# A bidirectional encoder layer: VectorE in place of GpSimd, four more products early, another order of products, and v loaded earlier

## The chip, the cores and the metric

The kernel runs on one core of a Trainium2 chip. The time is device microseconds of one execution; lower is better. The core's engines work at the same time, each through a queue of its own: TensorE (PE) multiplies matrices, VectorE (DVE), ScalarE (ACT) and GpSimd (POOL) do elementwise work, and SyncE (SP) issues most DMAs; POOL issues others. PE writes to PSUM, which has eight banks here: four under the name "g", four under "d".

## The reference

One layer on 1024 tokens of width 1024, all in float32:

```
h = x + 1/2 * SwiGLU_1(RMSNorm(x))                # d_ff 2816
u = RMSNorm(h)
[qA|kA|vA|qB|kB|vB|gA|gB] = u @ W_in
yA = NeighbourhoodAttention2D(qA, kA, vA)         # 8 heads, learned bias
yB = WindowedGQA(rope(qB), rope(kB), vB)          # 8 heads, 2 of k and v, sink logit
h = h + (sigmoid(gA)*(yA @ W_A) + sigmoid(gB)*(yB @ W_B)) @ W_out
h = h + 1/2 * SwiGLU_2(RMSNorm(h))
y = RMSNorm_final(h)
```

Scores of qA, kA and qB, kB are scaled by 0.125.

## The kernel before

**Arithmetic.** Each float32 operand is split into a high part (a ScalarE cast to fp32r, line 88) and a low part (a subtraction, line 89, by VectorE unless another engine is named). One product of such operands is three matmuls: high by high, high by low, low by high (`mm3`, lines 137 to 144).

**Products in Strassen form.** The gate and up projections of both FFNs and most of W_in are computed with seven products P1 to P7 in place of eight. The right-hand sides B11, B21, T2, T1, B22, T3 and T4 come from the normalized, transposed activations: T1 = B12 - B11, T2 = B22 - T1, T3 = T2 - B11, T4 = B21 - T2. In `to_strassen` (lines 188 to 218) token tiles 0 to 3 give B11 and B21, tiles 4 to 7 give B22, T1 and T2, and the corners that become T3 and T4, which `strassen_rest` (220 to 225) splits at the end. Of T1 the low part, and the two corner subtractions (lines 210, 211), are on GpSimd.

**`products`** (232 to 330) runs over groups i of output columns (11 for an FFN, 5 for W_in); in a group each product is done for m = 0 and 1 (gate and up, or two chunk pairs of W_in). A step (i, p, m) is four yields of three matmuls. W, X and Y are the PSUM banks of a group: P1, P6, P7, P4 add up in W, P2 in X, P5 and P3 in Y. Between them `after` copies or adds the banks out. `prep` loads and splits the left-hand side; `prep_until` sets how far ahead. P1 and P2 of group 1 are taken early, behind those of group 0, since they need only B11 and B21; `load_ahead` loads their weights. `hidden` (344 to 388) is the FFN's `after`, with SwiGLU and the left-hand sums of the down projection, written to DRAM by POOL DMAs; `store_z` (598 to 632) is that of W_in, which writes z to DRAM.

**Transitions.** `transition` (159 to 178) norms and transposes tile by tile; after tile t its `post(t - 1)` runs some yields of the early products (`behind`, 332 to 342: seven each from t = 3 on). There are three: before FFN1, before W_in (the mix stage), before FFN2. `fetch` (264 to 267) multiplies the weights of qA and qB (column chunks 0 to 3 and 12 to 15 of W_in) by 0.125 on GpSimd.

**Hooks.** In the W_in stage `at_end(n)` calls what is hooked to n products before the end: five `rope` steps (640 to 655: two `xs` buffers, loads from z, three VectorE operations, a POOL DMA) and `v_b` (657 to 668: loads v of B from z into an `xs` buffer and transposes it on PE). There are two `xs` buffers.

The order in each engine's queue is made at build time: instructions are taken as the builder thinks their inputs ready, earlier lines first.

Of the kernel before, what the change touches and what calls it, by code (L numbers as in the profile page):

```python
# [15 lines left out]
P = 128  # L16
# [20 lines left out]
def trunk_kernel(ctx, tc, x, n1, wg1, wu1, wd1, nm, win, rpb, sink, wa, wb, wo,  # L37
# [150 lines left out]
    def to_strassen(t, xs):  # L188

        pa, pb = turned(xs)  # L190
        tt = t % 4
        cols = slice(tt * P, (tt + 1) * P)

        def put(o, src, eng=None):
            h, l = rhs(o)
            split(h[:, :, cols], l[:, :, cols], src, eng)

        x11 = res(tt)[:, :512].rearrange("p (c t) -> p c t", c=4)
        x21 = res(tt)[:, 512:].rearrange("p (c t) -> p c t", c=4)
# [9 lines left out]
        nc.vector.tensor_tensor(t2, pb, t1, op=ALU.subtract)  # L209
        nc.gpsimd.tensor_tensor(x11, t2, x11, op=ALU.subtract)  # L210
        nc.gpsimd.tensor_tensor(x21, x21, t2, op=ALU.subtract)
        put(T2, t2)
        put(B22, pb)
        put(T1, t1, nc.gpsimd)
        if kept:
            x12 = main.tile([P, 512], F32, tag="s1", bufs=1, name=nm_("s1"))
            nc.scalar.copy(x12.rearrange("p (c t) -> p c t", c=4), pa)
            nc.sync.dma_start(kept[0][t - 4], x12)

    def strassen_rest():  # L220
        for o, k in ((T3, 0), (T4, 512)):
            h, l = rhs(o)
            for tt in range(4):
                cols = slice(tt * P, (tt + 1) * P)
                split(h[:, :, cols], l[:, :, cols], res(tt)[:, k:k + 512].rearrange("p (c t) -> p c t", c=4))
# [6 lines left out]
    def products(src, n, after, at_end, extra, ring, scaled=lambda i, m, half: False):  # L232

        seq = [(i, p, m) for i in range(n) for p in PRODUCTS for m in range(2)]
        early = [(1, p, m) for p in ("P1", "P2") for m in range(2)]
# [19 lines left out]
        def load_ahead():  # L258

            for m in range(2):  # L260
                ahead[m] = main.tile([P, 1024], F32, tag="ws", bufs=8, name=nm_("ahead"))
                fetch(ahead[m], 1, m, 0)

        def fetch(r, i, m, half):
            nc.sync.dma_start(r.rearrange("p (c f) -> p c f", f=P), src(i, m, half))
            if scaled(i, m, half):
                nc.gpsimd.tensor_scalar_mul(r, r, 0.125)

        def prep(q):
            if q >= len(seq):  # L270
                return
            i, p, m = seq[q]
            if (i, p, m) in early:
                w = lhs[q] = ws4()
                c0 = 512 if p == "P2" else 0
                split(w[:, :512], w[:, 512:], ahead[m][:, c0:c0 + 512])
                return
            for half in range(2):
                if (i, m, half) not in raws:
                    load(i, m, half)  # L280
            r1, r2 = raws[i, m, 0], raws[i, m, 1]
            a11, a12, a21, a22 = r1[:, :512], r1[:, 512:], r2[:, :512], r2[:, 512:]
            s1 = None
            if p == "P5":
                s1 = main.tile([P, 512], F32, tag="s1", bufs=1, name=nm_("s1"))
                nc.vector.tensor_tensor(s1, a21, a22, op=ALU.add)
            elif p == "P3":
                nc.vector.tensor_tensor(a12, a12, a11, op=ALU.subtract)
            w = ws4()
            split(w[:, :512], w[:, 512:], dict(P1=a11, P2=a12, P5=s1, P6=a11, P7=a21, P3=a12, P4=a22)[p])  # L290
            if p == "P5":
                nc.vector.tensor_tensor(a21, a11, a21, op=ALU.subtract)
                nc.vector.tensor_tensor(a11, s1, a11, op=ALU.subtract)
            lhs[q] = w

        def multiply(q):
# [13 lines left out]
            for c in range(4):  # L310
                cs = slice(c * P, (c + 1) * P)
                mm3([b], c == 0 and p in ("P1", "P2", "P5"), c == 3, (w[:, cs], w[:, 512:][:, cs]),
# [10 lines left out]
        def run():  # L323
            for q in range(len(seq)):
                prep_until(q + 1 if q < 4 else q + 8)
                yield from multiply(q)
                after(*seq[q], bks[seq[q][0]], snap[seq[q][0]], sn)
# [4 lines left out]
    def behind(prods):  # L332
# [3 lines left out]
        def post(t):  # L336
            if t >= 3:
                drain(run, 7)
# [5 lines left out]
    def hidden(wg, wu, at_end):  # L344
# [4 lines left out]
        def after(i, p, m, bks, snap, sn):  # L349
            if p in ("P1", "P6"):  # L350
                c = snap["11" if p == "P1" else "21", m] = sn()
                nc.scalar.copy(c, bks["W", m])
            elif p == "P5":
                c = snap["22", m] = sn()
                nc.scalar.copy(c, bks["Y", m])
            elif p == "P4":
                if m == 0:
                    snap["12"] = sn()
                    nc.scalar.activation(snap["12"], bks["W", 0], AF.Silu)
                    return  # L360
                a12, s4 = snap["12"], snap["21", 0]
                nc.vector.tensor_tensor(a12, bks["W", 1], a12, op=ALU.mult)
                put(i, "P2", a12)
                nc.vector.tensor_tensor(s4, a12, snap["21", 1], op=ALU.subtract)
                put(i, "P3", s4)
            else:
# [6 lines left out]
                g = snap[key, 0]  # L373
                nc.vector.tensor_tensor(g, c, g, op=ALU.mult)  # L374
                if p != "P3":
                    put(i, "P1" if p == "P2" else "P4", g)
                    return
                a11, a22 = snap["11", 0], snap["22", 0]
                s1, s2, s3 = snap["22", 1], c, snap["11", 1]
                nc.vector.tensor_tensor(s1, g, a22, op=ALU.add)  # L380
                put(i, "P5", s1)
                nc.vector.tensor_tensor(s2, s1, a11, op=ALU.subtract)
                put(i, "P6", s2)
                nc.vector.tensor_tensor(s3, a11, g, op=ALU.subtract)
                put(i, "P7", s3)
# [190 lines left out]
    drain(transition(res, gain, to_strassen, behind(hg), spare=(2, 3)))  # L576
# [21 lines left out]
    def store_z(i, p, m, bks, snap, sn):  # L598
# [9 lines left out]
        def put(ch, n, c):  # L608
            if ch < 12:
                parts = [(z_d, c)]  # L610
                if ch < 8:
                    hl = [main.tile([P, 512], F32R, tag="hs", bufs=4, name=nm_("hs")) for _ in range(2)]
                    split(hl[0], hl[1], c)
# [11 lines left out]
        if p in ("P1", "P5", "P6", "P4"):  # L625
            c = snap[key, m] = sn()
            nc.scalar.copy(shaped(c, ch), view(bks[src, m], ch))
        else:
            c = snap[key, m]
            nc.vector.tensor_tensor(shaped(c, ch), view(bks[src, m], ch), shaped(c, ch), op=ALU.add)  # L630
# [25 lines left out]

    def v_b():
        mix["vb"] = [new_fx(k, F32R).rearrange("p (t d) -> p t d", t=NTT) for k in (0, 1)]
        r = xs4()
        nc.sync.dma_start(r, z_d[17 * P:18 * P, :])  # L660
# [75 lines left out]
    for c in range(4):  # L736
        hook(14 * (NG - 1) - 2 - 3 * c, rope, c)
    hook(14 * (NG - 2) - 2, rope, 4)
    hook(14 * (NG - 2) - 12, v_b)
# [6 lines left out]
                  lambda i, m, half: groups[i][m][half] in (0, 1, 2, 3, 12, 13, 14, 15))  # L746
# [454 lines left out]
```

## Time and profile before

| | |
|---|---|
| median of 3 runs | 1987.9 us (1984.55 to 1991.54) |
| profiled execution, span | 1987.6 us |
| mean granted TensorE clock | 0.993 |
| DMA | 290.31 MB, 146 GB/s |
| PE, DVE, ACT, POOL busy | 98%, 72%, 48%, 21% of the span |

An engine's busy time counts the time in which at least one instruction of it was in work; matmuls overlap. A row of the windows view gives length, busy time and instruction count of PE, PE's weight loads, DVE, ACT and POOL, the granted clock as a share of the full one, and the DMA engines' share and rate. A row of waits names who waited for whom: total us, times, longest. A row of groups names line, engine, operation, what is written from what, count, busy us and mean ns, then idle time before it and who ended that. FFN1's transition and products fill about 0 to 440 us, the W_in stage about 640 to 870, FFN2's transition and products about 1320 to 1740; down projections and attention lie between.

### The profile page before, as it was taken

To read this page: it belongs to the slowest core of one execution; us is meant where nothing else is said; L and a number is where in the kernel's file an instruction comes from. 1 tells how busy PE (TensorE), PEld (TensorE's weight loads), DVE (VectorE), ACT (ScalarE), POOL (GpSimd) and SP (SyncE) were. 2 spreads that over 40 slices of the span, in tenths; PEclk is the share of its full clock that TensorE was granted. 3 is DMA by queue.
4 is the path that set the end of the run, shared out by engine and by line. 5 is a ranking of instruction groups with operands and counts; after the bars stand their busy time and mean duration, and the time that the engine had idled before them with its cause. 6 is when DMAs were issued, how large, how long until landed. Compare 5 with 4: busy or idle time off the path is not lost.

```text
span 1987.6 us, 25701 instructions
## 1 busy us (share of the span) xinstructions
PE 1938.4 (98%) x8968; PEld 1612.7 (81%) x8968; DVE 1439.8 (72%) x2495; ACT 957.4 (48%) x1857; POOL 422.0 (21%) x474
## 2 busy tenths in 40 slices
PE   6999999999999999999999999998999999999998
PEld 5788888888888778788888888887888888888886
DVE  7866566558967677768889866999656656659864
ACT  7433333334446443468777873365333333344453
POOL 4101001002500533311112134513101100105100
PEclk9999999999999999999999999999999999999999
DMA  6423323367233469973357675544332342393341
GB/s 194 147 85 106 121 92 106 108 220 277 84 121 125 145 160 243 201 174 107 87 143 173 172 253 195 179 147 127 120 114 88 105 126 85 125 349 129 108 140 62
DMA packets 257217, 290.31 MB, mean 146 GB/s; under 512 B 46880, under 2 KB 187552, under 8 KB 257088
## 3 DMA queue, kind: packets, MB, share of 16 engines
q1 hardware_dynamic: 200576, 203.09, 32.8%
q0 software_dynamic: 56512, 85.58, 15.2%
q8 instruction: 71, 1.16, 0.2%
q14 instruction: 58, 0.48, 0.1%
HBM read 202.01 MB, written 86.70 MB: 145 GB/s over the span
## 4 chain that ended last, share of the span: by engine, by line
PE 82%; DVE 8%; issue 4%; DMA 3%; POOL 2%; ACT 2%; SPq 0%; POOLq 0%; DVEq 0%; ACTq 0%
PE g L140 16%; PE g L142 16%; PE g L144 16%; PE d L140 10%; PE d L142 10%; PE d L144 10%; PE d L991 2%; DVE ws L89 2%; DVE ar L89 1%; DMA xs<-z_d 1%; PE d L970 1%; PE d L971 1%; PE g L1010 1%; PE g L1005 1%; DVE ar L1116 1%
## 5 line engine op out<-in xcount | busy, mean ns | idle before, releaser
L140 PE MATMUL g<-ar,ws 128*128 128x512 f32 x1208 | 455.7, 398 | 9.2 <-ACT ar L88 3.5
L142 PE MATMUL g<-ar,ws 128*128 128x512 f32 x1208 | 448.6, 392 | 3.7 <-DVE ar L89 3.7
L144 PE MATMUL g<-ar,ws 128*128 128x512 f32 x1208 | 447.3, 392 | 2.1 <-DVE ws L89 2.0
L89 DVE TENSOR_TENSOR ws<-raw,ws 128x512 fp32r<-128x512 f32 (+1 forms) x335 | 249.5, 748 | 189.6 <-ACT ws L88 188.4
L88 ACT CAST ws<-raw 128x512 fp32r<-128x512 f32 (+1 forms) x337 | 213.3, 638 | 272.6 <-PE d L144 108.5
L142 PEld LDWEIGHTS g<-ar,ws 128*128 128x128 f32 x1208 | 228.4, 189 | 52.0 <-DVE ar L89 4.4
L144 PEld LDWEIGHTS g<-ar,ws 128*128 128x128 f32 x1208 | 228.3, 189 | 51.7 <-DVE ws L89 3.2
L140 PEld LDWEIGHTS g<-ar,ws 128*128 128x128 f32 x1208 | 223.0, 189 | 51.9 <-ACT ar L88 4.7
L140 PE MATMUL d<-ar,ws 128*128 128x512 f32 x656 | 254.3, 392 | 4.7 <-DVE ar L89 4.7
L142 PE MATMUL d<-ar,ws 128*128 128x512 f32 x656 | 254.2, 391 | 0.0
L144 PE MATMUL d<-ar,ws 128*128 128x512 f32 x656 | 254.0, 391 | 0.0
L347 POOL DMA_DIRECT2D hid<-fx x98 | 53.1, 542 | 501.1 <-DVE fx L374 364.6
L140 PEld LDWEIGHTS d<-ar,ws 128*128 128x128 f32 x656 | 124.1, 189 | 31.4 <-issue 5.5
L144 PEld LDWEIGHTS d<-ar,ws 128*128 128x128 f32 x656 | 124.1, 189 | 25.9
L142 PEld LDWEIGHTS d<-ar,ws 128*128 128x128 f32 x656 | 124.0, 189 | 25.9
L89 DVE TENSOR_TENSOR ws<-ar,ws 128x512 fp32r<-128x512 f32 x114 | 109.1, 964 | 6.7 <-ACT ws L88 6.7
L89 DVE TENSOR_TENSOR ws<-fa,ws 128x512 fp32r<-128x512 f32 x80 | 55.3, 691 | 63.5 <-ACT ws L88 63.1
L88 ACT CAST ar<-raw 128x512 fp32r<-128x512 f32 (+1 forms) x83 | 56.0, 679 | 93.1 <-PE g L142 51.1
L140 PE MATMUL g<-ws,ws 128*128 128x512 f32 x232 | 90.9, 392 | 0.0
L142 PE MATMUL g<-ws,ws 128*128 128x512 f32 x232 | 90.4, 390 | 0.0
L144 PE MATMUL g<-ws,ws 128*128 128x512 f32 x232 | 90.3, 389 | 0.0
L978 ACT ACTIVATE fa<-fa,nmx 128x385 f32<-128x385 f32 (+3 forms) x128 | 75.5, 591 | 26.9 <-DVE nmx L975 26.2
(222 smaller groups left out, 3588.3 us busy)
## 6 DMA issues: line engine op xcount, KB each, us to landing
raw<-hid SPq DMA_DIRECT2D x70, 512.0 KB
hid<-fx POOLq DMA_DIRECT2D x98, 256.0 KB, 2.4
raw<-in_ffn_w_up_dram SPq DMA_DIRECT2D x32, 512.0 KB
ar<-in_ffn_w_down_dram SPq DMA_DIRECT2D x32, 512.0 KB
raw<-in_ffn_w_gate_dram SPq DMA_DIRECT2D x28, 512.0 KB
hid<-fa POOLq DMA_DIRECT2D x56, 256.0 KB, 2.7
raw<-in_w_in_dram SPq DMA_DIRECT2D x27, 512.0 KB
ar<-zs_d POOLq DMA_DIRECT2D x48, 256.0 KB, 5.0
```

The lines of the kernel that those rows point to most:

```text
L88: nc.scalar.copy(dst_hi, src)
L89: (eng or nc.vector).tensor_tensor(dst_lo, src, f32v(dst_hi), op=ALU.subtract)
L140: nc.tensor.matmul(b, lhs[0], r[0], start=first, stop=False, **kw)
L142: nc.tensor.matmul(b, lhs[0], r[1], start=False, stop=False, **kw)
L144: nc.tensor.matmul(b, lhs[1], r[0], start=False, stop=last, **kw)
L347: nc.gpsimd.dma_start(hid[PRODUCTS.index(p), i], src)
L970: nc.tensor.matmul(b[:, :nw], un["q"][s], un["kd"][s][:, k0 * P:k1 * P], start=True, stop=False)
L971: nc.tensor.matmul(b[:, :nw], un["q"][s], un["kl"][s][:, k0 * P:k1 * P], start=False, stop=True)
L978: nc.scalar.activation(pr, pr, AF.Exp, scale=-1.0, bias=nmx[:, s:s + 1], accum_out=ssum[:, s:s + 1])
L991: nc.tensor.transpose(pt[:, i * P:(i + 1) * P], un["pr"][s][:, i * P:(i + 1) * P], ident)
L1005: nc.tensor.matmul(o[:, s], un["v"][s][:, un["k0"] + i, :], un["p"][s][:, i], start=i == 0, stop=i == last)
L1010: nc.tensor.matmul(o, un["v"][0][:, un["k0"] + i, :], un["p"][k][:, i], start=i + k == 0, stop=i + k == last + 1)
```

## The change

- `to_strassen`: T1's low part and the corners go to VectorE; T1 is split first; corners of tiles 6 and 7 wait for `strassen_rest`.
- P3 comes before P7 (in the last group of W_in the old order stays); `hidden` builds its sums in the matching order.
- P1 and P2 of group 2 ("merged") are early too. They add up in one X bank; P1 alone is copied to a buffer `u`, and W then starts at P6, so that `u` is added where P6, P5 and P4 are read.
- `behind` runs 6, 9, 9, 8, 16 yields (FFN1: 7, 7, 7, 7, 20), 48 for the twelve early products; before it was 7 each, with 32 for eight.
- Splits run three products ahead at first and up to eight later; before, one ahead for four products, then eight at once.
- The factor 0.125 is taken at eviction, by ScalarE's scale or a VectorE operation with a scalar.
- v of B is loaded by a hook of its own, 14 products before its transposes; hooks move.

```
-        nc.gpsimd.tensor_tensor(x11, t2, x11, op=ALU.subtract)
-        nc.gpsimd.tensor_tensor(x21, x21, t2, op=ALU.subtract)
+        put(T1, t1)
         put(T2, t2)
         put(B22, pb)
-        put(T1, t1, nc.gpsimd)
+        if t < 6:
+            corners(tt)
...
+    def corners(tt):
+        x11, x21, t2 = res(tt)[:, :512], res(tt)[:, 512:], res(tt + 4)[:, 512:]
+        nc.vector.tensor_tensor(x11, t2, x11, op=ALU.subtract)
+        nc.vector.tensor_tensor(x21, x21, t2, op=ALU.subtract)
+
     def strassen_rest():
+        for tt in (2, 3):
+            corners(tt)
...
-    PRODUCTS = ("P1", "P2", "P5", "P6", "P7", "P3", "P4")
+    PRODUCTS = ("P1", "P2", "P5", "P6", "P3", "P7", "P4")
...
-        early = [(1, p, m) for p in ("P1", "P2") for m in range(2)]
+        early = [(i, p, m) for i in (1, MERGED) for p in ("P1", "P2") for m in range(2)]
...
+            for m in range(2):
+                for k, p in enumerate(("P1", "P2")):
+                    r = ahead[MERGED, p, m] = main.tile([P, 512], F32, tag="hs", bufs=4, name=nm_("ahead"))
+                    nc.sync.dma_start(r.rearrange("p (c f) -> p c f", f=P), src(MERGED, m, 0)[:, 4 * k:4 * k + 4, :])
...
-            if scaled(i, m, half):
-                nc.gpsimd.tensor_scalar_mul(r, r, 0.125)
...
-            if p in ("P1", "P6", "P7", "P4"):
-                if p == "P1":
+            if p == "P1" and i == MERGED:
+                b = bks[i]["X", m] = bank("d")
+            elif p in ("P1", "P6", "P7", "P4"):
+                if p == ("P6" if i == MERGED else "P1"):
                     bks[i]["W", m] = bank("g")
                 b = bks[i]["W", m]
+            elif i == MERGED and p == "P2":
+                b = bks[i]["X", m]
...
-                prep_until(q + 1 if q < 4 else q + 8)
+                prep_until(q + 3 if q < 8 else min(2 * q - 5, q + 8))
...
+                if i == MERGED and p == "P1":
+                    if m == 0:
+                        u = const.tile([P, 1152], F32, tag="gain", bufs=1, name=nm_("u"))
+                        c = xs4()
+                        for k in range(2):
+                            snap[i]["u", k] = u[:, k * 512:k * 512 + 512]
+                            snap[i]["11", k] = c[:, k * 512:k * 512 + 512]
+                    nc.scalar.copy(snap[i]["u", m], bks[i]["X", m])
...
-    def behind(prods):
+    def behind(prods, steps=(6, 9, 9, 8, 16)):
...
-                drain(run, 7)
+                drain(run, steps[t - 3])
...
+                if merged:
+                    nc.vector.tensor_tensor(c, bks[src, m], snap["u", m], op=ALU.add)
+                else:
+                    nc.scalar.copy(c, bks[src, m])
...
-            nc.scalar.copy(shaped(c, ch), view(bks[src, m], ch))
+            nc.scalar.activation(shaped(c, ch), bk, AF.Copy, scale=scale)
...
+    def v_b_load():
+        mix["vraw"] = xs4()
+        nc.sync.dma_start(mix["vraw"], z_d[17 * P:18 * P, :])
...
-        hook(14 * (NG - 1) - 2 - 3 * c, rope, c)
-    hook(14 * (NG - 2) - 2, rope, 4)
-    hook(14 * (NG - 2) - 12, v_b)
+        hook(14 * (NG - 1) - 6 - 3 * c, rope, c)
+    hook(14 * (NG - 2) - 6, rope, 4)
+    hook(14 * (NG - 2) - 8, v_b_load)
+    hook(14 * (NG - 2) - 22, v_b)
```

More of the change, by code (lines that the diff above doesn't have):

```diff
@@ L274, in prep @@
                 w = lhs[q] = ws4()
[L275 to L276 removed]
+                split(w[:, :512], w[:, 512:], ahead.pop((i, p, m)))
                 return
@@ L575, in trunk_kernel @@
         hg[0](0, m, 1)
-    drain(transition(res, gain, to_strassen, behind(hg), spare=(2, 3)))
+    drain(transition(res, gain, to_strassen, behind(hg, (7, 7, 7, 7, 20)), spare=(2, 3)))
     strassen_rest()
```

95 lines of the change are left out of this document (64 added, 31 removed).

## The prediction

> **What bounds the kernel now.** I read the page's first part, then the windows of the stretches in which TensorE (PE) does not keep its pace, then who PE waited for in each, and last the engine that is named there.
>
> ```profile
> PE 1938.4 (98%) x8968; PEld 1612.7 (81%) x8968; DVE 1439.8 (72%) x2495; ACT 957.4 (48%) x1857; POOL 422.0 (21%) x474
> ```
>
> PE is the bound, so an edit counts only by the PE idle time that it removes or adds. The next answer sets four stretches beside a steady one; its first columns are length, PE busy (matmuls), weight loads, VectorE (DVE), ScalarE (ACT), GpSimd (POOL), and after them the granted clock.
>
> ```profile
> 20.00:71.00 51.00, 43.57 (x180) 34.07 (x181) 48.78 (x65) 32.26 (x58) 22.96 (x17) 0.97 0.40 115
> 666.00:722.00 56.00, 49.83 (x215) 40.39 (x214) 45.48 (x59) 27.76 (x51) 33.63 (x27) 0.91 0.53 151
> 805.00:820.00 15.00, 10.49 (x40) 8.48 (x39) 6.75 (x11) 2.70 (x8) 1.21 (x2) 0.77 0.79 197
> 1319.00:1400.00 81.00, 74.35 (x348) 60.13 (x347) 78.24 (x111) 49.03 (x88) 27.16 (x24) 0.98 0.33 109
> 200.00:250.00 50.00, 50.00 (x223) 41.38 (x222) 28.39 (x43) 17.99 (x32) 4.34 (x8) 1.00 0.40 127
> ```
>
> The steady row gives the pace: 50 us for 223 matmuls, 0.224 us each, 2.7 us for a product of 12. There is nothing to win there. The three transitions (rows 1, 2 and 4: norm, transposes and right-hand splits of FFN1, mix and FFN2) and the transposes of v of B (row 3) leave PE idle for 51.00 - 43.57 = 7.4, 6.2, 4.5 and 6.7 us, 24.8 in all. A second loss lies in the clock. Three smaller windows show when:
>
> ```profile
> 60.00:65.00 5.00, 4.41 (x12) 3.51 (x13) 5.00 (x9) 1.77 (x3) 0.56 (x1) 0.66 0.63 181
> 1350.00:1360.00 10.00, 7.19 (x29) 5.56 (x27) 9.53 (x12) 6.71 (x11) 7.33 (x6) 0.83 0.30 99
> 1370.00:1375.00 5.00, 3.06 (x14) 2.25 (x13) 5.00 (x7) 2.15 (x4) 1.69 (x2) 1.00 0.28 81
> ```
>
> After idle spells of 2.7 and 2.8 us (below) the clock falls and costs 5 x 0.34 = 1.7 and 10 x 0.17 = 1.7 us; after 1.9 us (last row) it stays at 1.00. By (1 - clock) x length the mix transition loses 0.09 x 56 = 5.0 us, v of B 0.23 x 15 = 3.5. With 1.7 for each FFN, the clock costs 11.9 us, and idle and clock together **36.7 us**. That is all that this change can win in these places.
>
> [...]
>
> Who PE waited for in the three transitions (total, times, longest):
>
> ```profile
> PE d L140 <- DVE ar L89: 2.7, 1, 2.7
> PE d L133 <- DVE xs L124: 2.1, 3, 1.5
> PE g L144 <- DVE ws L89: 1.3, 1, 1.3
> PE g L140 <- ACT ar L88: 1.0, 2, 0.6
> PE g L140 <- DVE fa L369: 0.3, 1, 0.3
> ```
> ```profile
> PE g L142 <- DVE ar L89: 3.7, 1, 3.7
> PE g L140 <- ACT ar L88: 2.5, 1, 2.5
> ```
> ```profile
> PE g L140 <- DVE fa L369: 2.8, 1, 2.8
> PE d L140 <- DVE ar L89: 1.9, 1, 1.9
> PE g L140 <- ACT fx L352: 1.1, 2, 0.7
> PE g L144 <- DVE ws L89: 0.7, 1, 0.7
> ```
>
> In each, PE once ran out of early products before DVE had written the last low halves of T1, T2, B22 ("ar L89": 2.7, 3.7, 1.9 us). DVE is busy for 48.78 of 51 us and 78.24 of 81: it is what PE waits for.
>
> **GpSimd's bulk work to DVE.** What it removes:
>
> ```profile
> L267 POOL TENSOR_SCALAR raw<-raw 128x1024 f32<-128x1024 f32 x8 | 23.1, 2892 | 31.9 <-DMA raw<-in_w_in_dram 31.9
> L210 POOL TENSOR_TENSOR fx<-fa,fx 128x512 f32<-128x512 f32 x12 | 20.8, 1734 | 9.5 <-DVE fa L209 6.0 <-DVE st L121 3.4 <-ACT xs L118 0.2
> L211 POOL TENSOR_TENSOR fx<-fx,fa 128x512 f32<-128x512 f32 x12 | 20.0, 1667 | 0.0
> ```
>
> All three go, and the low half of T1 (12 more; the down projections' own POOL work stays). Per transition DVE gets 4 + 4 + 4 = 12 operations of 128x512. What they cost and what they give back stands in DVE's groups in 20 to 71 us:
>
> ```profile
> L89 DVE TENSOR_TENSOR ws<-raw,ws 128x512 fp32r<-128x512 f32 x11 | 8.3, 776 | 0.0
> L124 DVE SCALAR_TENSOR_TENSOR xs<-fa,st,gain 128x1024 f32<-128x1024 f32 x4 | 7.1, 1768 | 1.2 <-POOL st L122 1.2
> ...
> L89 DVE TENSOR_TENSOR ar<-fa,ar 128x512 fp32r<-128x512 f32 x4 | 4.8, 1208 | 1.1 <-ACT ar L88 1.1
> L89 DVE TENSOR_TENSOR ar<-d,ar 128x512 fp32r<-128x512 f32 x6 | 4.0, 679 | 0.0
> ...
> L288 DVE TENSOR_TENSOR raw<-raw 128x512 f32<-128x512 f32 x2 | 2.5, 1228 | 0.0
> L292 DVE TENSOR_TENSOR raw<-raw,raw 128x512 f32<-128x512 f32 x2 | 2.4, 1224 | 0.0
> ```
>
> The operations that read PSUM (ar<-d) take 679 ns. The same subtraction with both inputs in SBUF takes 1208 on average, and 1228 and 1224 elsewhere: they meet POOL's. The excess is 11 x 97 + 4 x 529 + 2 x 549 + 2 x 545 ns = 5.4 us, and for L124 4 x (1768 - 1284) = 1.9, where 1284 is the same operation's mean in the mix transition:
>
> ```profile
> L124 DVE SCALAR_TENSOR_TENSOR xs<-fa,st,gain 128x1024 f32<-128x1024 f32 x3 | 3.9, 1284 | 4.9 <-POOL st L122 4.9
> ```
>
> So 7.3 us come back for 12 x 0.68 = 8.2 added: DVE's load stays within 1 us. The mix row adds something: DVE stood idle for 4.9 us for the one-column power on POOL, queued behind bulk work; that queue goes, and with it the late release of a PSUM bank that I take to be behind the 2.5 us wait there (ACT named is the last by semaphore). The factor 0.125 of L267 moves into operations that exist, ScalarE copies and DVE additions; I take 0 for it: between products DVE waits for PE (0.89 us idle, below), so that even one operation more would be hidden.
>
> **Four more products early, in shared banks.** 4 x 12 matmuls x 0.224 = 10.8 us of PE work now lie ahead of the first need of T1. It is moved, not added. Its price: four more splits per transition (2.7 us of DVE, within the 10.8), four more 256 KB loads on SP's queue behind those of x, and in one group of eleven some six additions on DVE in place of ScalarE copies, where DVE is busy for 28.39 of 50 us: 0. The early pairs hold two of the four "d" banks that the transposes use; a wait for a bank costs what the FFN2 row shows, 0 to 2.8 us a stage and not below 0. I take 0, since pacing spreads DVE's queue, and keep 2.8 for the range. DVE has now 8.2 - 7.3 + 2.7 = 3.6 us more to do by a time 10.8 us later: the T waits (2.7, 3.7, 1.9) go, with 7 us to spare.
>
> **P3 ahead of P7** moves the need of T3 back by two products (5.4 us) and takes away the 1.1 us on L352, P7 behind the copy of P6's bank. It adds a wait: P4 of the first half follows P7 of the first half by one product, and DVE must have added that bank (L369) within 2.7 us. In steady state DVE stands ready:
>
> ```profile
> 404.98 0.69 DVE L369 TENSOR_TENSOR fx<-g,fx 128x512 f32<-128x512 f32 x1 [0.89 <-PE g L144]
> 405.69 0.69 DVE L89 TENSOR_TENSOR ws<-fa,ws 128x512 fp32r<-128x512 f32 x1
> ```
>
> It had idled 0.89 us for PE and took 0.69, so I price this at 0; what is queued behind a late addition is the next splits, and PE at P4.
>
> **Paced splits** move the burst of eight (at the fifth product) behind the norms of the last tiles. The waits on "ws L89" (1.3, 0.7) and the late L369 (2.8 with 1.7 of clock) are of that kind; they go for the most part. The waits of transposes on the norm (2.1) and on ACT (1.0) stay, as DVE stays full until the last tile.
>
> **v of B.** The rope steps share two buffers, and the load of v waits for one:
>
> ```profile
> 794.87 0.34 SPq L648 DMA_DIRECT2D xs<-z_d  x1
> ...
> 809.87 0.34 SPq L660 DMA_DIRECT2D xs<-z_d  x1
> ```
> ```profile
> PE g L664 <- DMA xs<-z_d: 4.5, 1, 4.5
> ```
>
> The last rope step's load goes out at 794.87 and v's 15.0 us later, as soon as a buffer is free, however early it is asked for. So the early request alone gains little. But the transposes move too: hooks are counted from the end, the rope steps' go from 2 to 6 products before their mark, which the four products moved ahead make up, and the transposes' from 12 to 22, so that they stand six products (16 us) later behind the last rope step than before; and P3's move ends the first rope input two products sooner. On SP's queue the load of v now stands ahead of later weight loads; held for a buffer it holds them for 15.0 us at most, and splits run eight products (21 us) ahead: 0. Between no gain and 8.0 us (4.5 and 3.5 of clock) I take 6.0, nearer to the full row, since 16 us are more than the 4.5 waited.
>
> **Sum.** FFN1: 2.7 + 1.7 clock + 1.3 + 0.8 of the other 3.4 = 6.5. Mix: 3.7 + 2.5 + 5.0 less 1.5 kept = 9.7. FFN2: 1.9 + 1.1, and 0.6 of the other (2.8 + 1.7 + 0.7), which is 3.1: 6.1. v: 6.0. Together 28.3. The profiled execution spans 1987.6, the median is 1987.9 (1984.55 to 1991.54), so they agree, and the forecast is 1987.9 - 28.3 = **1960** (1959.6).
>
> **Rivals.** *DVE stays the bound.* If the slow DVE operations do not speed up, each transition gets 8.2 + 2.7 us of DVE against 10.8 of cover: the T waits stay, and what is won is v of B (6.0), L352 (1.1) and the POOL queue of the mix (2.5 + 1.7): 11.3, **1977**. For it: DVE at 96%. Against it: the 679 beside 1208 ns. [...]
>
> *Nothing in sum.* The schedule put the transposes of v where the load was thought to be back, and may do so again; and "d" banks cost 3 x (2.8 + 1.7) = 13.5. With 28.3 - 6.0 - 13.5 = 9 left, and half of that lost to new waits in the starts, **1984**.
>
> *Slower: P4 behind P7's addition.* 11 + 11 groups of the FFNs and 4 of the mix have the new order. If five DVE operations are queued when P7's first half ends, the addition ends after 6 x 0.69 = 4.1 us, 1.4 later than P4 could start; 26 x 1.4 = 36 us more, 1960 + 36 = **1996**. It decides from 28.3 / 26 = 1.1 us a group, more than four operations in the queue. Against it: the 0.89 us of idle above.
>
> **Chances.** Forecast 0.65, DVE bound 0.17, nothing 0.09, slower 0.09. All losses gone is 1987.9 - 36.7 = 1951, the low end with 1 us for spread; the high end takes in the DVE case with two waits for a bank on top: 1977 + 2 x 2.8 = 1983. The forecast's own range is 1950 to 1972. About 0.3% (6 us) can be told from no change: faster than 1982 is 0.82, within 0.09, slower 0.09.
>
> **What would show it.** Right: POOL without 128x512 operations in the transitions; DVE's SBUF subtractions there at 0.68 us; windows of the same stages with PE idle under 3 us and clock 0.97 or more; no PE wait on "ar L89". Wrong: PE waits on a DVE addition at every P4 (matmuls short of 222 in 50 us in the steady part), waits of transposes or first products for "d" banks, or the v load still landing after its transposes.

## The result and the profile after

The changed kernel takes 1963.19 us (median of 4 runs, 1962.18 to 1964.35). The kernel before, its profiled run counted among them, takes 1987.43 (4 runs, 1984.55 to 1991.54). The ratio is 0.9877, with a 95% interval of 0.9865 to 0.9889: faster by 1.2%, or 24 us. The profiled execution of the changed kernel took 1962.87 us, and its span is 1961.1, 26.5 less than before.

First the busy row of the changed kernel's page: GpSimd is busy for 86 us less, VectorE for as long as before.

```profile
PE 1927.7 (98%) x8968; PEld 1605.7 (82%) x8968; DVE 1442.4 (74%) x2543; ACT 951.7 (49%) x1845; POOL 335.7 (17%) x429
```

The windows of the same stages in the changed kernel, which come up to 20 us earlier now (columns: length, PE busy, weight loads, DVE, ACT, POOL, granted clock, DMA share, GB/s): FFN1, the mix in two rows, v of B, FFN2.

```profile
20.00:71.00 51.00, 48.75 (x220) 39.63 (x221) 50.02 (x83) 35.27 (x64) 3.76 (x6) 1.00 0.47 131
650.00:706.00 56.00, 55.17 (x260) 45.76 (x259) 48.91 (x80) 33.89 (x62) 10.27 (x15) 1.00 0.53 146
706.00:740.00 34.00, 32.22 (x141) 25.98 (x141) 23.38 (x34) 11.33 (x20) 3.79 (x7) 1.00 0.87 247
780.00:830.00 50.00, 50.00 (x227) 41.47 (x226) 35.60 (x55) 23.50 (x43) 17.32 (x21) 1.00 1.30 235
1300.00:1381.00 81.00, 78.91 (x372) 64.54 (x371) 75.97 (x125) 50.60 (x92) 5.74 (x11) 1.00 0.33 105
```

Length less PE busy is PE's idle time: 2.2, 0.8 + 1.8, 0 and 2.1 us, and the clock is full in all of them. Beside what the same stages lost before, idle and clock together:

| stage | before | after | won | forecast |
|---|---|---|---|---|
| FFN1 | 9.1 | 2.2 | 6.9 | 6.5 |
| mix | 11.2 | 2.6 | 8.6 | 9.7 |
| v of B | 8.0 | 0 | 8.0 | 6.0 |
| FFN2 | 8.4 | 2.1 | 6.3 | 6.1 |
| sum | 36.7 | 6.9 | 29.8 | 28.3 |

Two of the figures before count some time twice, as the clock was already low for a part of the time in which PE stood idle: 0.21 x 4.51 us in the wait for v and 0.17 x 3.71 us in the mix, 1.6 us together. So some 28 us were won in these stages. The span fell by 26.5, so 2 us or so were lost elsewhere. One spell accounts for them, behind ScalarE's copies for the gate. Here are two windows, the first of the changed kernel and the second of before:

```profile
1140.00:1155.00 15.00, 13.11 (x56) 10.69 (x55) 9.54 (x16) 10.21 (x15) 5.50 (x4) 0.89 0.79 224
```
```profile
1160.00:1175.00 15.00, 13.66 (x70) 11.52 (x69) 9.75 (x21) 11.52 (x19) 9.23 (x5) 1.00 0.84 250
```

It was 1.3 us of idle time at full clock; now it is 1.9 us and 0.11 x 15 = 1.7 us of clock, so 2.2 more.

What PE still waits for in the three transitions of the changed kernel (total, times, longest):

```profile
PE g L144 <- DVE ws L89: 1.5, 1, 1.5
PE g L140 <- ACT ar L88: 0.6, 1, 0.6
...
```
```profile
PE g L140 <- DVE fa L690: 1.8, 2, 1.1
PE g L140 <- ACT ar L88: 0.8, 1, 0.8
```
```profile
PE g L140 <- DVE fa L413: 1.6, 1, 1.6
PE g L140 <- DVE fx L413: 0.4, 1, 0.4
```

"DVE ar L89", which cost 2.7, 3.7 and 1.9 us, is gone from the transitions. In FFN1 and FFN2 it was not an operand that PE had waited for. Here is the end of the wait in FFN1, before:

```profile
59.77 0.68 DVE L89 TENSOR_TENSOR ar<-d,ar 128x512 fp32r<-128x512 f32 x1
```
```profile
60.59 0.47 PE L140 MATMUL d<-ar,ws 128*128 128x512 f32 x1 [2.73 <-DVE ar L89]
```

A matmul of line 140 takes high halves alone, which ScalarE writes, and the subtraction that ended the wait (the low half of B22) reads a bank "d". So the wait was, as far as the rows tell, for the bank of the last transposes; in the mix it was for a low half (L142). I go on calling the three "T waits", as the prediction does. VectorE is late in all of them.

"fa L413", the addition of an early P2, is the late L369 of before (2.8 us there). "fa L690" and "fx L413" are new: additions of P7 that P4 waits for, at four places in the whole run (1.8 us here in the mix, 0.4 here and 0.6 later in FFN2) and not at each of 26 groups.

DVE's groups in 20 to 71 us of the changed kernel show the other sign that was looked for. Each 128x512 subtraction takes 0.69 us, where those with both inputs in SBUF took up to 1.21 before:

```profile
L89 DVE TENSOR_TENSOR ws<-raw,ws 128x512 fp32r<-128x512 f32 x10 | 6.4, 688 | 0.0
L89 DVE TENSOR_TENSOR ar<-fa,ar 128x512 fp32r<-128x512 f32 x8 | 5.5, 685 | 0.0
L89 DVE TENSOR_TENSOR ws<-ahead,ws 128x512 fp32r<-128x512 f32 x8 | 5.4, 687 | 0.0
L124 DVE SCALAR_TENSOR_TENSOR xs<-fa,st,gain 128x1024 f32<-128x1024 f32 x4 | 5.1, 1284 | 1.4 <-POOL st L122 1.2
```

### The profile page after: what moved, and what is told of

The parts are those of the page before. It is cut to its first block, busy times and chain, and to the rows that moved or that the text cites. A ratio compares the mean times of both kernels' runs of the same rounds, so it can differ in the third digit from the quotient of the medians.

```text
span 1961.1 us, 25643 instructions
## 1 busy us (share of the span) xinstructions
PE 1927.7 (98%) x8968; PEld 1605.7 (82%) x8968; DVE 1442.4 (74%) x2543; ACT 951.7 (49%) x1845; POOL 335.7 (17%) x429
## 5 line engine op out<-in xcount | busy, mean ns | idle before, releaser
L140 PE MATMUL g<-ar,ws 128*128 128x512 f32 x1184 | 444.7, 397 | 8.0 <-ACT xs L901 1.9
L142 PE MATMUL g<-ar,ws 128*128 128x512 f32 x1184 | 437.5, 391 | 0.6 <-DVE ar L89 0.6
L144 PE MATMUL g<-ar,ws 128*128 128x512 f32 x1184 | 435.7, 390 | 1.5 <-DVE ws L89 1.5
L89 DVE TENSOR_TENSOR ws<-raw,ws 128x512 fp32r<-128x512 f32 (+1 forms) x329 | 239.4, 733 | 180.7 <-ACT ws L88 179.4
L88 ACT CAST ws<-raw 128x512 fp32r<-128x512 f32 (+1 forms) x331 | 209.1, 638 | 289.3 <-PE d L144 129.6
L144 PEld LDWEIGHTS g<-ar,ws 128*128 128x128 f32 x1184 | 222.7, 188 | 49.0 <-DVE ws L89 1.9
L140 PE MATMUL d<-ar,ws 128*128 128x512 f32 x680 | 262.3, 390 | 0.0
L142 PE MATMUL d<-ar,ws 128*128 128x512 f32 x680 | 261.9, 389 | 0.0
L144 PE MATMUL d<-ar,ws 128*128 128x512 f32 x680 | 261.9, 389 | 0.0
L142 PEld LDWEIGHTS g<-ar,ws 128*128 128x128 f32 x1184 | 223.0, 188 | 47.4 <-DVE ar L89 1.1
L140 PEld LDWEIGHTS g<-ar,ws 128*128 128x128 f32 x1184 | 217.5, 189 | 51.0 <-ACT ar L88 4.2
L140 PEld LDWEIGHTS d<-ar,ws 128*128 128x128 f32 x680 | 127.7, 188 | 26.5
L144 PEld LDWEIGHTS d<-ar,ws 128*128 128x128 f32 x680 | 127.6, 188 | 26.4
L142 PEld LDWEIGHTS d<-ar,ws 128*128 128x128 f32 x680 | 127.7, 188 | 26.3
L89 DVE TENSOR_TENSOR ws<-ar,ws 128x512 fp32r<-128x512 f32 x114 | 108.1, 956 | 9.0 <-ACT ws L88 9.0
L89 DVE TENSOR_TENSOR ws<-fa,ws 128x512 fp32r<-128x512 f32 x76 | 52.5, 691 | 57.7 <-ACT ws L88 57.4
L142 PE MATMUL g<-ws,ws 128*128 128x512 f32 x232 | 90.4, 390 | 0.0
```

The lines of the kernel that those rows point to most:

```text
L88: nc.scalar.copy(dst_hi, src)
L89: (eng or nc.vector).tensor_tensor(dst_lo, src, f32v(dst_hi), op=ALU.subtract)
L140: nc.tensor.matmul(b, lhs[0], r[0], start=first, stop=False, **kw)
L142: nc.tensor.matmul(b, lhs[0], r[1], start=False, stop=False, **kw)
L144: nc.tensor.matmul(b, lhs[1], r[0], start=False, stop=last, **kw)
```

## The experiments

The total was as forecast, but a total can be right by the wrong parts. My theory was the prediction's list: GpSimd's work costs VectorE about what it gives back, the cover of four more early products takes away the T waits, pacing the waits for splits, and a later place the wait for v. The rival: nearly all of it is VectorE no longer colliding with GpSimd. Each run is compared with runs of the kernel before on the same chip. Comparisons across chips go by those ratios, since the changed kernel itself gave 0.9877 and, on another chip, 0.9867.

### GpSimd's bulk work alone, in the kernel before

T1's low half and the corners go to VectorE, T1 first, the corners of tiles 6 and 7 behind the transition; all else stays.

```
-        nc.gpsimd.tensor_tensor(x11, t2, x11, op=ALU.subtract)
-        nc.gpsimd.tensor_tensor(x21, x21, t2, op=ALU.subtract)
+        put(T1, t1)
         put(T2, t2)
         put(B22, pb)
-        put(T1, t1, nc.gpsimd)
+        if t < 6:
+            corners(tt)
...
     def strassen_rest():
+        for tt in (2, 3):
+            corners(tt)
```

> The kernel before with one part of the change alone: T1's low part and the corners on VectorE, corners of tiles 6 and 7 in the rest, T1 split first; all else as before (1987 us), the scaling of the weights on GpSimd too. Theory: VectorE does the twelve operations in the time that the collisions took, the mix transition loses the wait of 2.5 us and its clock, the waits for T1, T2 and B22 stay in part since nothing new covers them: -4 to -9 us, 1978 to 1983. Rival, the collisions were the main cause of the old waits: -12 us or more, 1975 or less. Rival, VectorE is the bound and takes longer by 8.2 us in each transition: slower than 1990.

Measured: 1975.22 us (1972.95 to 1975.37), ratio 0.9935 (0.9917 to 0.9952), 11.6 us under the kernel before on that chip. It is near the rival's number, and it has a loss in it: PE now waits 6.9 us for v, not 4.5. Here are its windows of FFN1, mix and FFN2, and PE's waits over its whole run:

```profile
20.00:71.00 51.00, 47.18 (x200) 37.59 (x201) 46.88 (x77) 32.20 (x58) 3.24 (x5) 0.97 0.42 115
666.00:722.00 56.00, 54.34 (x249) 44.08 (x248) 49.87 (x81) 30.39 (x57) 21.79 (x18) 1.00 0.67 187
1300.00:1381.00 81.00, 78.10 (x373) 63.85 (x372) 75.40 (x124) 51.86 (x94) 6.06 (x11) 1.00 0.43 140
```
```profile
PE g L671 <- DMA xs<-z_d: 6.9, 1, 6.9
PE g L144 <- DVE ws L89: 4.2, 4, 2.9
...
PE d L140 <- DVE ar L89: 1.0, 1, 1.0
```

Of the T waits (8.3 us) 1.0 is left, without a single product more of cover. With the clock at 0.97 in the first window, the three stages lose 5.3, 1.7 and 2.9 us, where they lost 9.1, 11.2 and 8.4.

Why VectorE is in time can be read in its timeline of this kernel, in the mix:

```profile
693.12 0.68 DVE L89 TENSOR_TENSOR ar<-fa,ar 128x512 fp32r<-128x512 f32 x1
693.72 1.28 DVE L89 TENSOR_TENSOR ws<-raw,ws 128x512 fp32r<-128x512 f32 x2
694.92 0.68 DVE L89 TENSOR_TENSOR ar<-d,ar 128x512 fp32r<-128x512 f32 x1
...
700.36 0.68 DVE L222 TENSOR_TENSOR fx<-fa,fx 128x512 f32<-128x512 f32 x1
700.96 0.69 DVE L223 TENSOR_TENSOR fx<-fx,fa 128x512 f32<-128x512 f32 x1
```

The corners of tiles 6 and 7 (L222, L223) come behind the last low halves of T ("ar"). So 8 operations stand ahead of T's need, not 12: 8 x 0.69 = 5.5 us against the 7.3 that come back. VectorE is 1.8 us ahead, and in the mix by another 4.1, as its wait for the power on GpSimd falls from 5.6 to 1.5 (640 to 740 us, four operations; the 4.9 of the prediction's row are those of three):

```profile
L124 DVE SCALAR_TENSOR_TENSOR xs<-fa,st,gain 128x1024 f32<-128x1024 f32 x4 | 5.1, 1280 | 1.5 <-POOL st L122 1.5
```

1.8, 5.9 and 1.8 us stand beside T waits of 2.7, 3.7 and 1.9. By this sum the four corners that stand behind the transition are 2.8 us of it (4 x 0.69); no run separates the collision from the order of the corners.

### The same part undone, in the changed kernel

The corners (all tiles, ahead of the splits) and T1's low half go back to GpSimd; cover, pacing, order and v stay as changed.

```
-        put(T1, t1)
+        corners(tt)
         put(T2, t2)
         put(B22, pb)
-        if t < 6:
-            corners(tt)
+        put(T1, t1, nc.gpsimd)
...
-        nc.vector.tensor_tensor(x11, t2, x11, op=ALU.subtract)
-        nc.vector.tensor_tensor(x21, x21, t2, op=ALU.subtract)
+        nc.gpsimd.tensor_tensor(x11, t2, x11, op=ALU.subtract)
+        nc.gpsimd.tensor_tensor(x21, x21, t2, op=ALU.subtract)
...
     def strassen_rest():
-        for tt in (2, 3):
-            corners(tt)
```

> The changed kernel with one part undone: T1's low part and all corner subtractions are on GpSimd again, in the old order within a tile. Everything else stays as changed (1963.2 us). My theory: VectorE's load in a transition is the same within 1 us (8.2 us taken away, about 7 us of collisions back), and the waits for T1, T2, B22 have some 7 us to spare, so they stay away; what comes back is the wait for the one-column power behind GpSimd's queue in the mix transition (up to 2.5 + 1.7 us) and a part of the small waits: +2 to +6 us, 1965 to 1969. In the profile VectorE's subtractions with two SBUF inputs in the transitions are above 1 us again on the mean. Rival, the collisions are the main cause of the old waits: +12 us or more, 1975 and up, with PE waits on 'ar L89' back. Second rival, a full VectorE is the bound and moving work to it cost something: at or below 1963.

Measured: 1976.14 us (1975.56 to 1976.83), ratio 0.9937 (0.9922 to 0.9952): half of the gain is lost, which is again the rival's size. Here are VectorE's groups in 20 to 71 us of this kernel, and after them PE's waits in its mix (650 to 730) and in its FFN2 transition (1310 to 1391):

```profile
L89 DVE TENSOR_TENSOR ws<-ahead,ws 128x512 fp32r<-128x512 f32 x8 | 8.2, 1039 | 0.0
L89 DVE TENSOR_TENSOR ws<-raw,ws 128x512 fp32r<-128x512 f32 x7 | 6.7, 994 | 0.0
...
L89 DVE TENSOR_TENSOR ar<-fa,ar 128x512 fp32r<-128x512 f32 x4 | 5.4, 1351 | 0.0
```
```profile
PE d L140 <- ACT u L345: 1.9, 2, 1.2
PE g L140 <- ACT ar L88: 1.2, 1, 1.2
PE d L140 <- DVE ar L89: 0.8, 1, 0.8
```
```profile
PE g L140 <- DVE fa L410: 3.9, 2, 2.8
PE d L140 <- DVE ar L89: 1.1, 1, 1.1
PE d L140 <- ACT u L345: 1.1, 1, 1.1
```

The subtractions are back at 1.0 to 1.35 us. "DVE ar L89" is back with 0.8 and 1.1 us, in front of matmuls of line 140 into "d" banks, as in FFN1 and FFN2 of the kernel before. But it stands at an earlier product: P1 of the merged group starts in a bank that the transposes held until VectorE has split B22, and its P2 waits for ScalarE's copy `u` of that bank. These come due before T1 does. The early products in shared banks brought a due time of their own, and VectorE keeps it only without GpSimd beside it. The largest, 3.9 us in two parts in FFN2, is for the addition of an early P2 (L410), for which PE waited 1.6 us in the changed kernel. By idle time and clock the three transitions lose 4.7, 5.0 and 6.9 us here, against 2.2, 2.6 and 2.1.

### Without the merged group

Group 1 alone is early, with the old number of yields and the hooks set back by four.

```
-    MERGED = 2
+    MERGED = -1
...
-        early = [(i, p, m) for i in (1, MERGED) for p in ("P1", "P2") for m in range(2)]
+        early = [(i, p, m) for i in (1,) for p in ("P1", "P2") for m in range(2)]
...
-    def behind(prods, steps=(6, 9, 9, 8, 16)):
+    def behind(prods, steps=(7, 7, 7, 7, 7)):
...
```

> The changed kernel with one part undone: only group 1's P1 and P2 are early, no shared bank, seven yields after each tile, hooks set back by the four products. My theory: 10.8 us of cover are gone from each transition, and the waits for T1, T2 and B22 come back in part, as VectorE is now paced: between half and all of 2.7 + 3.7 + 1.9 us with up to 3 x 1.7 of clock, +6 to +13 us, 1969 to 1976; v of B stays hidden. Rival, the old waits came from collisions with GpSimd and from the burst of splits alone: within 2 us of 1963.

Measured: 1975.16 us (1974.07 to 1976.39), ratio 0.9932 (0.9917 to 0.9947). The size was as my theory expected, the cause was not: the T waits stayed away. PE's wait over the whole run, and VectorE's timeline ahead of the longest one (3.8 us, ended at 62.87):

```profile
PE g L144 <- DVE ws L89: 8.1, 4, 3.8
```
```profile
57.30 4.91 DVE L89 TENSOR_TENSOR ar<-fx,ar 128x512 fp32r<-128x512 f32 x8
62.12 0.70 DVE L89 TENSOR_TENSOR ws<-raw,ws 128x512 fp32r<-128x512 f32 x1
```

The paced order puts the left-hand split of a product behind eight low halves of T3 and T4 (4.9 us). With four products less ahead of it, PE is there first. FFN2 has the same wait (3.2 us).

### Without the pacing

```
-                prep_until(q + 3 if q < 8 else min(2 * q - 5, q + 8))
+                prep_until(q + 1 if q < 4 else q + 8)
```

> The changed kernel with one part undone: splits run one product ahead for the first four products and then eight ahead at once. My theory: the burst falls between the norms of the last tiles again, and waits on 'ws L89', on late additions that free a bank and on the norm come back: +2 to +6 us, 1965 to 1969. Rival, with the collisions gone VectorE gets through the burst in time: within 1.5 us of 1963. If banks of group d are then short at the new early products, more than +6.

Measured: 1967.64 us (1966.3 to 1968.34), ratio 0.9893 (0.9878 to 0.9908), 3 to 4 us above the changed kernel, within what was expected. PE waits 3.3 us on "ws L89", 2.9 of them at once:

```profile
PE g L144 <- DVE ws L89: 3.3, 2, 2.9
```

So the wait for splits is 4.2 us with neither cover nor pacing (the first run, which also has the old order of products), 8.1 with pacing alone, 3.3 with cover alone, 1.5 with both (0.5 when the changed kernel was run again). The two are worth little or less than nothing one by one. From the first run to the changed kernel on the same chip (1961.09) are 14.1 us. Of them v is 6.9 us and 1.6 of clock behind its wait (0.30 x 5.22), and the spell at the gate's copies is 2.3: it took 2.4 us with 1.5 of clock behind it in the first run, and 1.6 us at full clock in the changed kernel there. That leaves 3 to 4 us for cover, pacing and P3's place together.

### P7 before P3 again, run twice

```
-    PRODUCTS = ("P1", "P2", "P5", "P6", "P3", "P7", "P4")
+    PRODUCTS = ("P1", "P2", "P5", "P6", "P7", "P3", "P4")
```

`hidden` builds its sums in the matching order.

> The changed kernel with one part undone: P7 before P3 in every group, with the FFN's sums in the order that this needs. My theory: the wait of P7 for the copy of P6's bank comes back (about 1.1 us), the wait of P4 for the addition of P7's bank goes (2.8 us in the changed profile: 1.8 in the mix stage, 1.0 in FFN2), T3 is needed 5.4 us earlier but is ready: 1961 to 1965, no difference that can be told. Rival, T3 and T4 decide the end of the transitions: +4 us or more, with PE waiting on 'ar L89' at P7.

> The changed kernel as it is, on the same chip as the next run, for a direct comparison: about 1963.

> The changed kernel with P7 before P3 again, beside the changed kernel on one chip. Its first run gave 1960.0, 3 us under the changed kernel's 1963.2 on another chip. Theory: the new order trades 1.1 us of waits (P7 behind the copy of P6's bank) for 2.8 us (P4 behind the addition of P7's bank: 1.8 in the mix stage, 1.0 in FFN2), and T3 is ready in time either way: 1 to 3 us faster than the changed kernel. Rival, the 3 us were the chip: within 1 us of it. It is the fastest version so far if the theory holds.

Measured: 1960.0 us (1958.97 to 1962.66), ratio 0.9854 (0.9837 to 0.987). On another chip, beside the changed kernel: 1959.28 (1957.85 to 1960.67; 0.9857, 0.9839 to 0.9875) against 1961.09 (1960.33 to 1962.4; 0.9867, 0.985 to 0.9884). It is lower both times, with intervals that overlap: P3's place brings no gain that can be measured, and may cost 2 us. The waits of P4 on P7's addition go, and T3 is ready in time in the old order too. P7's wait for the copy of P6's bank (1.1 us on L352 before) does not come back in either run of it. What grows is a wait outside the transitions, for the split of an attention operand at 867 us: 2.5 and 2.6 us, 0.6 and 0.7 in the changed kernel. This is the fastest version that was run.

### v of B: the early request and the place, one by one

The first kernel sets the request back to where the transposes are asked for, the second sets the transposes six products earlier.

```
-    hook(14 * (NG - 2) - 8, v_b_load)
+    hook(14 * (NG - 2) - 22, v_b_load)
```
```
-    hook(14 * (NG - 2) - 22, v_b)
+    hook(14 * (NG - 2) - 16, v_b)
```

> The changed kernel with one part undone: the load of v of B is asked for with its transposes instead of 14 products earlier; the transposes stay at their new place. My theory: the load waits for a rope buffer either way (in the changed profile it goes out at 795.07, 17.7 us after the last rope step's load and 8.8 us before the transposes), so asking early gains only what lies between the buffer coming free and the hook: within 2 us of 1963, PE waiting at most 2 us for z_d. Rival, the early load is what removed the wait: PE waits 4.5 us or more for xs<-z_d again with a slow clock behind it, 1969 to 1972.

> The changed kernel with one part undone: the transposes of v go back to their old distance behind the last rope step (six products earlier), with the load still asked for at its new place, eight products ahead. My theory: the place is what counts; the transposes are ordered ahead of the load's landing again and PE waits 2 to 4.5 us with up to 3.5 us of clock: +2 to +8, 1965 to 1971. Rival, the early load is enough, or the order at build time sets the transposes back by itself: within 1.5 us of 1963.

Measured: 1961.7 us (1960.43 to 1962.79), ratio 0.9874 (0.9859 to 0.9888), and 1962.62 (1961.37 to 1964.48), ratio 0.9877 (0.986 to 0.9893). Neither changes the time, though the second was expected to cost 2 to 8 us. Here are the first rope load, the load of v and the transposes, first in the changed kernel, then in the one with the earlier place:

```profile
718.91 0.34 SPq L708 DMA_DIRECT2D xs<-z_d  x1
...
795.07 0.34 SPq L719 DMA_DIRECT2D xs<-z_d  x1
...
803.90 1.03 PE L727 MATMUL g<-ident,xs 128*128 128x128 f32 x8
```
```profile
719.12 0.34 SPq L708 DMA_DIRECT2D xs<-z_d  x1
...
795.57 0.34 SPq L719 DMA_DIRECT2D xs<-z_d  x1
...
799.63 1.06 PE L727 MATMUL g<-ident,xs 128*128 128x128 f32 x8 [1.24 <-DMA xs<-z_d]
```

With the late request the load goes out at 794.11, no later than with the early one. From the first rope load to that of v the chain takes 76.2 us in the changed kernel, 76.5 with the earlier place and 75.7 in the kernel before (734.21 to 809.87), and about 4 us later the data are there (PE's wait for them ends at 813.79 before and at 799.63 with the earlier place, 3.9 and 4.1 us later). What differs is when PE comes to the transposes, counted from the first rope load: before at 75.1 us (813.79 less the wait of 4.51, less 734.21), with the earlier place at 79.3, in the changed kernel at 85.0. The 80 us needed explain all three: waits of 4.5, 1.2 and none. So the place it is, by 9.9 us, as these times argue; no run brought the whole wait back. Six products back gave only 5.7 of them, as the build sorts the queues by its own estimate.

### GpSimd beside VectorE: three probes

For each of the tiles 4 to 7 of a transition the changed kernel gets more GpSimd work that nobody needs: three subtractions of 128x512, three memsets of 128x512, or twelve subtractions of 128x96. The first two write into T4's space, which then still holds operands of the last down-projection products, so these products work on other values in both.

```
+        for _ in range(3):
+            dump = ar[T4][:, 0, :512]
+            nc.gpsimd.tensor_tensor(dump, gain[:, :512], gain[:, 512:], op=ALU.subtract)
```
```
+            nc.gpsimd.memset(f32v(dump), 0.0)
```
```
+        dump = main.tile([P, 96], F32, tag="dump", bufs=1, name=nm_("dump"))
+        for _ in range(12):
+            nc.gpsimd.tensor_tensor(dump, res(t)[:, 512:608], res(t)[:, :96], op=ALU.subtract)
```

> The changed kernel with work added: in each of the tiles 4 to 7 of a transition GpSimd runs three subtractions of 128x512 on two SBUF inputs (two halves of the norm's gain) into space that is overwritten later. VectorE's work is unchanged, nothing waits for the results. Theory after the run with GpSimd's work back (+13 us): the collisions are what costs, VectorE's two-input operations go above 1 us and the banks of group d come free too late for the shared pairs: +8 to +20, 1971 to 1983. Rival, the cost there was the longer way through GpSimd (T1's low half and the corners late): within 2 us of 1963.

> As the run with added GpSimd subtractions, but each is a memset of 128x512, which reads no SBUF. Theory: VectorE's two-input operations collide with GpSimd's reads, so that a memset leaves them at 0.68 us: within 2 us of 1963. [...] Rival, any GpSimd operation holds VectorE up: as much as with the subtractions, in proportion to the memset's duration.

> The changed kernel with work added: after each of the tiles 4 to 7 of a transition GpSimd runs twelve subtractions of 128x96 on two SBUF inputs (parts of T2 and T1 of this tile) into a scratch tile that nobody reads. VectorE's and ScalarE's work is unchanged and nothing waits for the results, so this has the collisions without the longer way through GpSimd. Theory, collisions cost: VectorE's two-input operations in the transitions rise above 0.69 us and PE waits for low halves and for banks of group d come back, +5 to +15 us, 1968 to 1978. Rival, the way through GpSimd is what cost 13 us when its work was put back: within 2 us of 1963. The power operation of the norms queues behind this work too; its wait is told apart in the profile.

Measured: 1990.29 us (1988.91 to 1992.83; ratio 1.0019, 1.001 to 1.0029), 1964.73 (1963.5 to 1967.95; 0.9892, 0.9877 to 0.9907) and 1984.47 (1983.08 to 1986.28; 0.9982, 0.9972 to 0.9993). The total of the first settles nothing: its operations stood in GpSimd's queue ahead of the norm's power, and PE waited up to 11.1 us behind that. The small ones cost more than the 5 to 15 us expected. Here are VectorE's groups with them in 20 to 71 us:

```profile
L89 DVE TENSOR_TENSOR ws<-ahead,ws 128x512 fp32r<-128x512 f32 x8 | 6.4, 809 | 0.0
...
L124 DVE SCALAR_TENSOR_TENSOR xs<-fa,st,gain 128x1024 f32<-128x1024 f32 x4 | 5.1, 1286 | 3.8 <-POOL st L122 3.8
```

Both effects are there, 809 against 687 ns and 3.8 against 1.2 us of idle time for the power, so this stage doesn't separate them. The total shows that 12 x 12 GpSimd operations whose results no one uses take back 21 to 23 of the 24 us.

FFN2's transition separates them better. Here are PE's longest wait in it (1317 to 1400) and VectorE's waits for the power up to there, with the small operations (1317 to 1354) and in the changed kernel (1295 to 1332):

```profile
PE g L140 <- DVE fa L416: 4.1, 1, 4.1
```
```profile
DVE xs L124 <- POOL st L122: 1.2, 2, 0.7
```
```profile
DVE xs L124 <- POOL st L122: 1.0, 2, 0.7
```

PE waits 4.1 us for an addition for which it waited 1.6, with almost the same idle time for the power. From the first subtraction of tile 4 (L208) to the end of that addition VectorE takes 20.1 us (1333.10 to 1353.18), and 17.5 in the changed kernel (1313.53 to 1330.99). Of the 2.6 us more, 0.7 are waits and 1.9 are slower operations.

That they are slower beside GpSimd can be read from the starts and ends of the operations in the traces. VectorE's 128x512 operations with both inputs in SBUF that overlap with GpSimd's bulk operations by more than 0.1 us take 1344 ns on average in the kernel before (135 of them; the 1089 others 691), 1345 beside the subtractions of the first probe (11) and 807 beside the small ones (88). Beside a memset there were only four, of 684 to 693 ns, as the memsets ran early. So VectorE's operations with both inputs in SBUF were slower beside GpSimd's bulk operations and its small subtractions, 1.34 and 0.81 us in place of 0.69. That a GpSimd operation which only writes leaves them alone was a guess ahead of these runs, and four operations are weak evidence for it.

## Why the prediction was right, and where it was not

**The total and the stages** were right: 1963 for 1960, and each stage within 2.0 us of its term. The idle time kept in the transitions is small, and the high end was not needed. The 36.7 us that could be won were 35.1, as 1.6 us of low clock fell into idle time that was counted already.

**GpSimd's work to VectorE, priced as neutral for VectorE.** This step failed. The 7.3 us that come back were right (0.69 us an operation now). But "8.2 added" counted all twelve operations ahead of T's need, and four of them stand behind it; and the idle time for the power counted only for one bank wait. The part alone is worth 11.6 us although it lengthens the wait for v by 2.4, and undoing it costs about 12.

**Four more early products: "the T waits go, with 7 us to spare".** They go, but not by this. The first run has none of the cover and 1.0 of 8.3 us left; two of the three were waits for a bank, which VectorE frees sooner when it is quick. What the cover does is carry the paced splits over T3 and T4, which the prediction did not see: without it they are late by 3.8 and 3.2 us. The shared banks, priced at 0 to 2.8 us a stage, cost nothing as long as VectorE is quick. With GpSimd's work back they cost 2.7 us in the mix and 2.2 in FFN2, so 0 was right, but not for the pacing's sake, which that run has as well.

**Paced splits.** "ws L89" went from 1.3 and 0.7 to 1.5 and none, and the late L369 of 2.8 is a late L413 of 1.6. "For the most part" was too much, but the part is worth the 3 to 4 us that it was given, beside the cover.

**P3 ahead of P7, priced at 1.1 gained and 0 lost.** The other way by a little. The 1.1 us are gone with the old order too, so P3's place did not take them away; it brought 1.8 + 1.0 us of new waits (L690, fx L413), and no gain was measured. The rival's mechanism is real, at four places: VectorE is free at nearly every P4, as the 0.89 us of idle time had said.

**v of B** went as told: the request brings nothing, the place all of it. The six products were taken for 16 us behind the last rope step and were 12.1 (14.4 us from that step's load before, 26.5 now), or 9.9 from the first rope load, which was enough; 6.0 for a wait that went whole was too careful.

**The clock term** (11.9 us, 1.6 of them in idle time) went from the stages as told; 1.7 us came up at the gate's copies. As a rule of the wait's length it was wrong (last section).

The parts do not add up: 12 for GpSimd's work, 11 for the cover, 3 for the pacing and 8 for v, each taken away from the changed kernel or read in its stage, are 34 us for a change of 24. The prediction's sum came out because it was bounded by the idle time and clock of each stage, and not by the prices of the parts. The T waits were credited to the cover and went by GpSimd's part; that this left the sum as it was is luck.

## What to carry to other kernels

Sum a change of many parts by what each stage can win, and take the price of a part as a guess until it was run alone and undone: here each half of a pair (cover and pacing, shared banks and a quick VectorE) was worth little or a loss without the other. Where an engine is full, look first at what runs beside it, for its own operations may be slower by it (here 1.34 us on average in place of 0.69), and count only those new operations that stand ahead of the next need. For a wait on a chain, count from the chain's first step to the consumer's place, not from one product to another.

## What the runs showed of the hardware

In these runs the clock after an idle spell of PE did not go by the spell's length alone. I listed the spells of 1.5 us or more (from 10 us on) in nine traces: before, the changed kernel (twice), the old order (twice), GpSimd's part alone and undone, no merged group, no pacing. All eight of 1.51 to 1.60 us left the clock at full; all five of 3.2 to 6.9 us were followed by some 3 us at 0.50 to 0.72; of the fifteen between 1.86 and 2.90 us nine were followed by such a fall and six were not. The other five traces, from 30 us on, are alike: no fall after three of 1.5 to 1.7 us, one after each of five of 4.1 to 11.1, and after four of seven between 1.8 and 2.6.

What tells the falls apart in these traces is where the spell lies. In the kernel before, the clock falls at 60.95, 689.00, 702.65, 811.88 and 1354.60 us, which are 184, 4, 32 and 159 steps of 3.413 us apart; no longer step fits them all. It stays at 0.50 for one step (3.41 us), or for two (6.83 us) from 702.65 and from 811.88, where PE was busy for 63 and 44% of the first. In each of the fourteen traces all falls (37 together, with those after the last matmul) lie on one such grid, to within 3 ns; where the grid begins differs from run to run (2.92 us behind the span's start before, 3.17 in the changed kernel). I divided each trace by its grid into windows. In the window ahead of each fall PE was busy for at most 47% of the time. Of the 7881 windows at full clock with no fall behind them, two were below 48%, at 43 and 44%. Here are two windows of the changed kernel, with the spell of 1.89 us that ends at 1146.46 (the wait for the gate's copies), and two of the kernel with the old pacing, with a spell of 2.90 us that ends at 36.04:

```profile
1143.23:1146.64 3.41, 1.52 (x9) 1.20 (x8) 1.73 (x5) 3.36 (x6) 2.65 (x2) 1.00 0.93 265
1146.64:1150.06 3.42, 3.42 (x9) 2.64 (x9) 3.37 (x4) 1.22 (x3) 2.55 (x2) 0.50 0.52 192
```
```profile
31.67:35.08 3.41, 1.46 (x11) 1.09 (x9) 3.41 (x7) 3.40 (x8) 0.00 (x0) 1.00 0.05 5
35.08:38.49 3.41, 2.45 (x11) 2.04 (x12) 3.28 (x6) 1.57 (x3) 0.55 (x1) 1.00 0.02 7
```

The shorter spell lies in one window, leaves PE 45% of it and costs a window at half clock. The longer one is shared by two windows, leaves 43 and 72%, and costs nothing; the first of these is one of the two exceptions. So these figures show no sharp border: falls behind windows of 45 and up to 47%, none behind two of 43 and 44%. The prediction took its rows for a rule of length (a fall after 2.7 and 2.8 us, none after 1.9), but in these traces the length alone does not tell.
